# Attention inside a transformer block: weight subtractions in pieces, a copied key half, softmax sums moved into the head's norm

## The chip, the cores and the metric

The kernel runs on one core of a Trainium2 chip. The metric is the time of one execution in device microseconds, the median of several runs. One of the executions is also recorded by the hardware profiler: for every engine it shows when each instruction began and how long it took, and which event ended its wait. Engines are named as the profile names them: PE (TensorE, matrix products and transposes), DVE (VectorE), ACT (ScalarE), POOL (GpSimd) and SP (SyncE, whose queue starts the transfers of weights). L12 is line 12 of the kernel.

## What is computed

One transformer block on 512 tokens of width 1024, in float32. A normalized input is projected by one wide matrix into the queries, keys and values of a differential attention of 8 heads, the latents of a second attention of 8 heads (MLA), and two gates. The first attention weighs two softmax maps, the second with a factor, and normalizes each head's output:

```python
for q, k, c in zip(q_maps, k_maps, coefs):        # coefs = [1.0, -lam]
    s = jnp.einsum('bqhd,bkhd->bhqk', q[:, q0:q1], k[:, :q1], ...) * scale
    p = jax.nn.softmax(jnp.where(mask, s, -jnp.inf), axis=-1) * c
    w = p if w is None else w + p
...
o = rms_norm(o, subln_g) * (1.0 - lambda_init)    # over the 128 columns of a head
```

The gated outputs of both attentions are added, multiplied by w_o and added to the input; then a router picks 2 of 32 experts for each token, in 4 groups, and the experts' gated feed-forward networks (1024 to 512 to 1024) are added.

## The kernel before

**Two-part products.** Matrix products of the attention keep nearly full float32 precision by splitting each operand into a high part, rounded to the matrix engine's format (F32R), and a low part, the rest. `mm3` (L89) then makes three products. `load_split` (L287) does this for weights: SP's queue brings a piece `wraw` of 128 rows by several slices k of n columns (usually four slices of 256 columns, 1024 elements a partition), ACT casts it to `whi` (L298), POOL subtracts, `wlo = wraw - whi` (L299). There are two buffers of `wraw` and four each of `whi` and `wlo`. 72 such pieces are loaded up to some 530 us; other widths are 704, 768, 512 and 384.

**Stages.** ORDER is a string of steps in program order: `q`, `k`, `v` project queries, keys and values of two heads at once; `fq`, `fk` normalize and rotate them (`rope`, L350; `rsqrt`, L95, makes 1/sqrt by a shift, a constant and three rounds of Newton's iteration in a dozen small DVE operations); `st` transposes them and splits them into stacks (`da_stacks`, L481); `h` is one head (`da_head`, L508); `sub` the norms of four heads together (`subln`, L530); `g` and `mg` gates; names with m the same for the second attention; `wo` the first part of the output product. Then come the router and the experts, in 16 pairs, whose weights stream through a ring of buffers by SP's queue (L879). A scheduler takes the program order and, by its own estimate of times, sets the order of instructions on every engine; waits between engines are semaphores derived from what the instructions read and write.

**The keys' stack.** For each of two maps `da_stacks` writes the key's high part twice, into both halves of the 128 partitions (two ACT operations, L501 and L502, out of PSUM), and the low part twice (two DVE operations, L504, also out of PSUM).

**The softmax.** `attend` (L362) goes through four query tiles of 128. For each tile and map PE makes the scores `pss`, DVE adds the mask and takes the row's extreme `nm` (L378), ACT makes the exponentials `e` and their sums `l` (L382). Then DVE takes reciprocals `r` of both sums (L387), multiplies the second by the factor `nlam` (L391), scales the second map (L392), and combines it with the first, scaled in the same operation (L393). PE transposes the result (L398), ACT and DVE split it into `pth` and `ptl` (L82, L83 in `split`), and PE multiplies by the values (L91 to L93). For the second attention, with one map, there is only a reciprocal and one scaling (L395).

**The norm of the heads.** Each head's output `po` is copied, squared and summed over its columns by a product with ones; after four heads `subln` transposes the four sums into a PSUM tile `pt`, `rsqrt` turns them into factors (L100 is its first operation), and each head is scaled.

Of the kernel before, what the change touches and what calls it, by code (L numbers as in the profile page):

```python
# [11 lines left out]
F32 = mybir.dt.float32  # L12
# [10 lines left out]
P = 128  # L23
T = 512
NT = T // P
# [4 lines left out]
EPS = 1e-6  # L30
# [38 lines left out]
class Kernel:  # L69
# [24 lines left out]

    def rsqrt(self, ss, n, scale, pool, tag, out=None):  # L95

        v = self.v
        tags = tag and (tag + "x", tag + "y", tag + "a")
        x, y, a = pool if tag is None else (pool.tile([P] + n if isinstance(n, list) else [P, n], F32, tag=tg, name="rs") for tg in tags)
        v.tensor_scalar(x, ss, scale, EPS, op0=mult, op1=add)  # L100
        yi = y.bitcast(I32)
# [160 lines left out]
    def attention(self):  # L262
# [24 lines left out]
        def load_split(src, nk, n, step, then=(), into=None):  # L287

            w, then = [], list(then)
            for k0 in range(0, nk, step):  # L290
                k1 = min(nk, k0 + step)
                hi = wp.tile([P, k1 - k0, n], F32R, tag="whi", name="whi", bufs=4)
                lo = wp.tile([P, k1 - k0, n], F32R, tag="wlo", name="wlo", bufs=4)
                raw = wp.tile([P, k1 - k0, n], F32, tag="wraw", name="wraw", bufs=2) if into is None else into
                self.last_load = nc.sync.dma_start(raw, src(k0, k1))
                if then:
                    then.pop(0)()
                s.copy(hi, raw)  # L298
                g.tensor_tensor(lo, raw, hi.bitcast(F32), op=sub)  # L299
                w += [(hi[:, k, :], lo[:, k, :]) for k in range(k1 - k0)]  # L300
            return w
# [59 lines left out]

        def attend(scores, scale, vh, vl, po):  # L362
            for hf in range(2):
# [5 lines left out]
                for qi in range(2):  # L369
# [4 lines left out]
                    for m, sc in enumerate(scores):  # L374
# [7 lines left out]
                        s.activation(e[:, 0:nk], pss[:, 0:nk], AF.Exp, scale=-1.0, bias=nm,  # L382
                                     accum_out=l[:, m:m + 1])
                        es.append(e)
                    r = sm.tile([P, 2], F32, tag="r", name="r", bufs=6)
                    n = len(scores)
                    v.reciprocal(r[:, 0:n], l[:, 0:n])  # L387
                    w = es[0][:, 0:nk]
                    if n == 2:
                        e2 = es[1][:, 0:nk]  # L390
                        v.tensor_tensor(r[:, 1:2], r[:, 1:2], self.nlam, op=mult)  # L391
                        v.tensor_scalar(e2, e2, r[:, 1:2], None, op0=mult)  # L392
                        v.scalar_tensor_tensor(w, w, r[:, 0:1], e2, op0=mult, op1=add)  # L393
                    else:
                        v.tensor_scalar(w, w, r[:, 0:1], None, op0=mult)  # L395
                    pt = tps()
# [84 lines left out]
        def da_stacks(hh, q, k):  # L481
# [16 lines left out]
            for m in range(2):  # L498
# [3 lines left out]
                s.activation(kh[b], pk[a], AF.Copy, scale=gk[a])  # L502
                for c in (a, b):
                    v.scalar_tensor_tensor(kl[c], pk[a], gk[a], kh[a].bitcast(F32), op0=mult, op1=sub)  # L504
                ks.append((kh, kl))
            return qs, ks

        def da_head(pr, hh, qs, ks, vv):  # L508
# [9 lines left out]
            po = ps.tile([P, T], F32, tag="O", name="po")  # L518
            attend([mk(0), mk(1)], 64 ** -0.5, lambda kt: vv[0][:, kt, hc], lambda kt: vv[1][:, kt, hc], po)
            o2 = main.tile([P, T], F32, tag="e", name="o2", bufs=4)  # L520
# [3 lines left out]
            pe.matmul(pso[0:32], self.ones, o2, start=True, stop=True)  # L524
            j = h % 4
            if j == 0:
# [3 lines left out]
        def subln(h0):  # L530
# [3 lines left out]
            ss = pt.rearrange("p t (j c) -> p t j c", j=4)[:, :, :, 0]  # L534
            r = self.rsqrt(ss, [NT, 4], 1.0 / P, sm, "rn")
            for j in range(4):
# [793 lines left out]
```

## Time and profile before

| | |
|---|---|
| median of 3 runs | 1081.29 us (1081.0 to 1082.02) |
| profiled execution | 1079.62 us, of which the recorded span is 1077.9 us |
| PE busy | 974.9 us (90%) |
| DVE busy | 512.3 us (48%) |
| ACT busy | 371.5 us (34%) |
| POOL busy | 204.4 us (19%) |
| mean granted clock of PE | 0.959 of full speed |
| DMA, mean over the span | 236 GB/s |

The shares are means over stages that differ: DVE does most of its work before 530 us, the transfers of the experts' weights fill the time after it. A line of the profile that groups instructions gives their number, the busy time in all, the mean of one, and the idle time of the engine in front of them with the instruction that ended it. A row of the timeline gives start, duration, engine, line, operation, the tile written and those read, and the shape; in brackets stands idle time in front of it.

### The profile page before, as it was taken

How to read it: one execution, taken by the hardware profiler on the slowest of the kernel's cores; microseconds unless marked ns; L12 is line 12 of the kernel's file. 1: busy time of each engine (PE TensorE's matmuls, PEld its weight loads, DVE VectorE, ACT ScalarE, POOL GpSimd, SP SyncE). 2: the span in 40 equal slices, each digit the busy share in tenths (PEclk: the TensorE clock that was granted, in tenths of full speed). 3: DMA queues.
4: the chain of work that ended last, by engine and by line, in shares of the span. 5: the costliest groups of instructions: out<-in, count | busy, mean ns of one | idle time of the engine just before them, and what ended most of it. 6: DMA issues, size and time to landing. Idle time of an engine off the chain costs nothing. (4 is left out here: it accounts for less than half of the span.)

```text
span 1077.9 us, 15395 instructions
## 1 busy us (share of the span) xinstructions
PE 974.9 (90%) x5718; PEld 687.1 (64%) x5718; DVE 512.3 (48%) x1512; ACT 371.5 (34%) x783; POOL 204.4 (19%) x218
## 2 busy tenths in 40 slices
PE   6798999999899799989989799999697979969795
PEld 6798988999678688879975354455252633525233
DVE  3878597694969889796463221211030110301012
ACT  5465555746765556645171111101010101101010
POOL 5333233313423222322230000000000000000001
PEclk9999999999999999999979899999898989989898
DMA  6321222112311211244687999999999999999995
GB/s 173 115 79 40 79 79 79 41 42 67 101 48 53 62 54 38 59 163 148 280 320 317 399 377 417 408 403 402 401 401 402 419 402 404 403 402 402 421 356 180
DMA packets 83708, 254.25 MB, mean 236 GB/s; under 512 B 12464, under 2 KB 47024, under 8 KB 65968
## 3 DMA queue, kind: packets, MB, share of 16 engines
q1 hardware_dynamic: 77504, 238.56, 57.6%
q0 software_dynamic: 2704, 9.96, 4.2%
q10 hardware_dynamic: 3424, 4.72, 1.2%
q8 instruction: 46, 0.75, 0.3%
q14 instruction: 30, 0.25, 0.1%
HBM read 240.64 MB, written 12.58 MB: 235 GB/s over the span
## 5 line engine op out<-in xcount | busy, mean ns | idle before, releaser
L1152 PE MATMUL pw<-w,xT 128*64 128x512 f32 x1024 | 250.4, 619 | 39.1 <-DMA w<-in_w_dram 36.7
L1152 PEld LDWEIGHTS pw<-w,xT 128*64 128x64 f32 x1024 | 81.8, 142 | 198.5 <-issue 155.9
L299 POOL TENSOR_TENSOR wlo<-wraw,whi 128x1024 fp32r<-128x1024 f32 (+4 forms) x70 | 149.6, 2147 | 233.9 <-ACT whi L298 233.0
L1161 DVE TENSOR_TENSOR hg<-pw,hg 128x512 f32<-128x512 f32 x16 | 16.7, 1041 | 277.3 <-PE pw L1152 276.5
L91 PE MATMUL pmm<-whi,hTh 128*128 128x256 f32 (+1 forms) x448 | 129.9, 293 | 2.1 <-ACT raw L465 1.8
L92 PE MATMUL pmm<-wlo,hTh 128*128 128x256 f32 (+1 forms) x448 | 129.2, 290 | 0.0
L93 PE MATMUL pmm<-whi,hTl 128*128 128x256 f32 (+1 forms) x448 | 127.2, 291 | 0.0
L1180 PE MATMUL py<-w,hT 128*64 128x512 f32 (+1 forms) x544 | 115.4, 572 | 1.4 <-ACT hT L1166 1.4
L1209 POOL DMA_INDIRECT obuf<-y,rows x15 | 23.5, 1570 | 462.8 <-DVE y L1184 136.3
L91 PEld LDWEIGHTS pmm<-whi,hTh 128*128 128x128 f32 x448 | 85.0, 190 | 3.5 <-ACT raw L465 2.2
L92 PEld LDWEIGHTS pmm<-wlo,hTh 128*128 128x128 f32 x448 | 85.2, 190 | 1.9 <-issue 1.7
L93 PEld LDWEIGHTS pmm<-whi,hTl 128*128 128x128 f32 x448 | 83.7, 190 | 1.1 <-issue 0.8
L1160 ACT ACTIVATE hg<-pw 128x512 f32<-128x512 f32 x16 | 17.0, 1064 | 194.8 <-PE pw L1152 156.7
L1180 PEld LDWEIGHTS py<-w,hT 128*64 128x64 f32 x544 | 42.5, 138 | 65.4 <-issue 56.9
L298 ACT CAST whi<-wraw 128x1024 fp32r<-128x1024 f32 (+4 forms) x70 | 65.0, 931 | 21.4 <-DMA wraw<-in_w_in_dram 6.1
L382 ACT ACTIVATE e<-pss,nm 128x128 f32<-128x128 f32 (+3 forms) x96 | 50.7, 532 | 62.5 <-DVE nm L378 32.3
L1166 ACT COPY hT<-pt 128x512 f32<-128x512 f32 x16 | 9.4, 586 | 163.6 <-PE pt L1164 163.6
L1020 PE MATMUL pg<-sel,hTh 128*128 128x256 f32 x256 | 65.6, 293 | 0.0
L1021 PE MATMUL pg<-sel,hTl 128*128 128x256 f32 x256 | 64.2, 290 | 0.0
L1184 DVE TENSOR_SCALAR y<-py,ws 128x512 f32<-128x512 f32 x15 | 11.2, 747 | 87.2 <-PE py L1180 87.2
L93 PE MATMUL pg<-hTh,wlo 128*128 128x512 f32 x128 | 51.1, 399 | 0.0
L91 PE MATMUL pg<-hTh,whi 128*128 128x512 f32 x128 | 50.9, 398 | 0.0
(344 smaller groups left out, 1920.0 us busy)
## 6 DMA issues: line engine op xcount, KB each, us to landing
w<-in_w_dram SPq DMA_DIRECT2D x138, 1024.0 KB, 16.8
w<-in_w_dram SPq DMA_DIRECT2D x106, 512.0 KB, 14.7
wraw<-in_w_in_dram SPq DMA_DIRECT2D x38, 512.0 KB, 3.7
wraw<-in_w_in_dram SPq DMA_DIRECT2D x8, 352.0 KB, 4.1
obuf<-X ACTq DMA_DIRECT2D x5, 512.0 KB
wraw<-in_mla_w_ukv_dram SPq DMA_DIRECT2D x4, 512.0 KB
wraw<-in_w_o_dram SPq DMA_DIRECT2D x4, 512.0 KB
X<-in_x_dram SPq DMA_DIRECT2D x4, 512.0 KB
```

Of the source, the lines that this page charges most:

```text
L91: self.pe.matmul(out, a[0], b[0], start=first, stop=False)
L92: self.pe.matmul(out, a[0], b[1], start=False, stop=False)
L93: self.pe.matmul(out, a[1], b[0], start=False, stop=last)
L298: s.copy(hi, raw)
L299: g.tensor_tensor(lo, raw, hi.bitcast(F32), op=sub)
L382: s.activation(e[:, 0:nk], pss[:, 0:nk], AF.Exp, scale=-1.0, bias=nm, accum_out=l[:, m:m + 1])
L1020: self.pe.matmul(pg, self.h2h[:, t, k, :], sel, start=t == 0 and k % 2 == 0, stop=False, skip_group_check=True)
L1021: self.pe.matmul(pg, self.h2l[:, t, k, :], sel, start=False, stop=t == NT - 1 and k % 2 == 1, skip_group_check=True)
L1152: end = pe.matmul(p[i * C:(i + 1) * C], xT[:, k, cols[i]], w(name, i, k), start=k == 0, stop=k == KT - 1)
L1160: s.activation(ha, ph[0][0:R].rearrange("p (a k) -> p a k", k=4), AF.Silu)
L1180: pe.matmul(p[i * C:(i + 1) * C], hT[:, k, i * C:(i + 1) * C], w("w2", i, k, c0, m), start=k == 0, stop=k == 3)
L1209: g.indirect_dma_start(self.obuf, bass.IndirectOffsetOnAxis(ap=rows, axis=0), yy, None, bounds_check=T + P - 1, compute_op=add)
```

## The change

Three things are changed. In `load_split` POOL's one subtraction for a loaded piece becomes one for each of its slices k: 72 instructions become 232, of 256 columns mostly (176), and of 128, 352, 384 or 512 where the loads are of that width. In `da_stacks` DVE makes the keys' low part once for each map, and ACT copies it to the other half of the partitions (new line L508). In `attend`, for the first attention, the first map is no longer divided by its sum: its sums go to a tile `l4` that is kept for four heads (one buffer), the second map is multiplied by `l1 * nlam / l2` and added to the unscaled first one in a single operation. As the head's output is then too large by the factor l1, and a norm follows that divides by the root of the mean square plus EPS, only EPS has to be multiplied by l1 squared: `subln` makes `EPS * l4 * l4`, and `rsqrt` adds that in place of the constant. The functions below keep their order otherwise; lines of the new kernel are some 3 to 9 higher.

```diff
@@ -92,12 +92,15 @@
         self.pe.matmul(out, a[0], b[1], start=False, stop=False)
         self.pe.matmul(out, a[1], b[0], start=False, stop=last)
 
-    def rsqrt(self, ss, n, scale, pool, tag, out=None):
+    def rsqrt(self, ss, n, scale, pool, tag, out=None, eps=None):
 
         v = self.v
         tags = tag and (tag + "x", tag + "y", tag + "a")
         x, y, a = pool if tag is None else (pool.tile([P] + n if isinstance(n, list) else [P, n], F32, tag=tg, name="rs") for tg in tags)
-        v.tensor_scalar(x, ss, scale, EPS, op0=mult, op1=add)
+        if eps is None:
+            v.tensor_scalar(x, ss, scale, EPS, op0=mult, op1=add)
+        else:
+            v.scalar_tensor_tensor(x, ss, scale, eps, op0=mult, op1=add)
         yi = y.bitcast(I32)
         v.tensor_scalar(yi, x.bitcast(I32), 1, None, op0=OP.logical_shift_right)
         v.tensor_scalar(yi, yi, -1.0, 1597463007.0, op0=mult, op1=add)
@@ -296,7 +299,8 @@
                 if then:
                     then.pop(0)()
                 s.copy(hi, raw)
-                g.tensor_tensor(lo, raw, hi.bitcast(F32), op=sub)
+                for k in range(k1 - k0):
+                    g.tensor_tensor(lo[:, k], raw[:, k], hi[:, k].bitcast(F32), op=sub)
                 w += [(hi[:, k, :], lo[:, k, :]) for k in range(k1 - k0)]
             return w
 
@@ -359,7 +363,9 @@
             v.tensor_tensor(out, xv, tb(cg, 0, 2 * h), op=mult)
             v.tensor_tensor(out, out, b, op=add)
 
-        def attend(scores, scale, vh, vl, po):
+        def attend(scores, scale, vh, vl, po, l0=None):
+
+
             for hf in range(2):
                 nkt = 2 * hf + 2
                 pth = main.tile([P, nkt, 256], F32R, tag=f"pth{hf}", name="pth")
@@ -380,19 +386,17 @@
                                                op0=add, op1=OP.min, accum_out=nm)
                         e = main.tile([P, T], F32, tag="e", name="e", bufs=4)
                         s.activation(e[:, 0:nk], pss[:, 0:nk], AF.Exp, scale=-1.0, bias=nm,
-                                     accum_out=l[:, m:m + 1])
+                                     accum_out=l[:, m:m + 1] if l0 is None or m else l0[qt])
                         es.append(e)
                     r = sm.tile([P, 2], F32, tag="r", name="r", bufs=6)
-                    n = len(scores)
-                    v.reciprocal(r[:, 0:n], l[:, 0:n])
                     w = es[0][:, 0:nk]
-                    if n == 2:
-                        e2 = es[1][:, 0:nk]
-                        v.tensor_tensor(r[:, 1:2], r[:, 1:2], self.nlam, op=mult)
-                        v.tensor_scalar(e2, e2, r[:, 1:2], None, op0=mult)
-                        v.scalar_tensor_tensor(w, w, r[:, 0:1], e2, op0=mult, op1=add)
+                    if l0 is None:
+                        v.reciprocal(r[:, 0:1], l[:, 0:1])
+                        v.tensor_scalar(w, w, r[:, 0:1], None, op0=mult)
                     else:
-                        v.tensor_scalar(w, w, r[:, 0:1], None, op0=mult)
+                        v.reciprocal(r[:, 0:1], l[:, 1:2])
+                        v.scalar_tensor_tensor(r[:, 1:2], r[:, 0:1], l0[qt], self.nlam, op0=mult, op1=mult)
+                        v.scalar_tensor_tensor(w, es[1][:, 0:nk], r[:, 1:2], w, op0=mult, op1=add)
                     pt = tps()
                     for kt in range(qt + 1):
                         pe.transpose(pt[:, kt, :], w[:, kt * P:(kt + 1) * P], ident)
@@ -500,8 +504,8 @@
                 kh, kl = stk("kh"), stk("kl")
                 s.activation(kh[a], pk[a], AF.Copy, scale=gk[a])
                 s.activation(kh[b], pk[a], AF.Copy, scale=gk[a])
-                for c in (a, b):
-                    v.scalar_tensor_tensor(kl[c], pk[a], gk[a], kh[a].bitcast(F32), op0=mult, op1=sub)
+                v.scalar_tensor_tensor(kl[a], pk[a], gk[a], kh[a].bitcast(F32), op0=mult, op1=sub)
+                s.copy(kl[b], kl[a].bitcast(F32))
                 ks.append((kh, kl))
             return qs, ks
 
@@ -516,13 +520,16 @@
                     pe.matmul(p[:, 0:n], qq, ks[m][1][:, 0:n], start=False, stop=True)
                 return sc
             po = ps.tile([P, T], F32, tag="O", name="po")
-            attend([mk(0), mk(1)], 64 ** -0.5, lambda kt: vv[0][:, kt, hc], lambda kt: vv[1][:, kt, hc], po)
+            j = h % 4
+            if j == 0:
+                self.l4 = sm.tile([P, NT, 4], F32, tag="l4", name="l4", bufs=1)
+            attend([mk(0), mk(1)], 64 ** -0.5, lambda kt: vv[0][:, kt, hc], lambda kt: vv[1][:, kt, hc], po,
+                   [self.l4[:, t, j:j + 1] for t in range(NT)])
             o2 = main.tile([P, T], F32, tag="e", name="o2", bufs=4)
             s.activation(o2, po, AF.Square)
             s.copy(mixed[:, h, :], po)
             pso = ps.tile([P, T], F32, tag="O", name="pso")
             pe.matmul(pso[0:32], self.ones, o2, start=True, stop=True)
-            j = h % 4
             if j == 0:
                 self.s4 = dp.tile([P, T], F32, tag="s4", name="s4")
             s.copy(self.s4[32 * j:32 * j + 32], pso[0:32])
@@ -532,7 +539,9 @@
             for t in range(NT):
                 pe.transpose(pt[:, t, :], self.s4[:, t * P:(t + 1) * P], ident)
             ss = pt.rearrange("p t (j c) -> p t j c", j=4)[:, :, :, 0]
-            r = self.rsqrt(ss, [NT, 4], 1.0 / P, sm, "rn")
+
+            v.scalar_tensor_tensor(self.l4, self.l4, EPS, self.l4, op0=mult, op1=mult)
+            r = self.rsqrt(ss, [NT, 4], 1.0 / P, sm, "rn", eps=self.l4)
             for j in range(4):
                 pb = ps.tile([P, T], F32, tag="O", name="pb")
                 for t in range(NT):
```

The scheduler places the new instructions. On DVE, for the first query tile of head 0, from a pair of key operations to the combination of the two maps, there stands before:

```order
L504 SCALAR_TENSOR_TENSOR kl<-pt,dagck,kh 64x512 x2
L378 ISA pss,nm<-pss,mask 128x256
L378 ISA nm 128x1
L387 RECIPROCAL r<-l 128x2
L426 TENSOR_REDUCE ssq<-sq 128x4
L391 TENSOR_TENSOR r<-r,nlam 128x1
L602 TENSOR_TENSOR ssq<-ssq,rx_343 128x16
L392 TENSOR_SCALAR e<-e,r 128x128
L100 TENSOR_SCALAR rs<-ssq 128x16
L393 SCALAR_TENSOR_TENSOR e<-e,r 128x128
```

and now (L507 is the key operation, L384 mask and extreme, L397 the reciprocal, L398 the factor, L399 the combination, L101 the first operation of `rsqrt`):

```order
L507 SCALAR_TENSOR_TENSOR kl<-pt,dagck,kh 64x512
L384 ISA pss,nm<-pss,mask 128x256
L384 ISA nm 128x1
L397 RECIPROCAL r<-l 128x1
L398 SCALAR_TENSOR_TENSOR r<-r,l_851,nlam 128x1
L399 SCALAR_TENSOR_TENSOR e<-e,r 128x128
L430 TENSOR_REDUCE ssq<-sq 128x4
L611 TENSOR_TENSOR ssq<-ssq,rx_355 128x16
L101 TENSOR_SCALAR rs<-ssq 128x16
```

The combination stands two places behind the reciprocal, where it stood six places behind; the sums of the projection (L430) and the small operations of the norm come after it.

On DVE, some 290 us into the kernel, heads 6 and 7 run beside the second attention's first steps. There stands before, from the copy of a rotated key (L591) to an operation of a norm's Newton iteration behind a pair of key operations:

```order
L591 COPY krd<-ckv 128x512
L111 TENSOR_TENSOR rs<-rs 128x4
L113 SCALAR_TENSOR_TENSOR rs<-rs 128x4
L378 ISA pss,nm<-pss,mask 128x128
L378 ISA nm 128x1
L112 TENSOR_TENSOR rs<-rs 128x4
L582 TENSOR_TENSOR r_4031<-rs 128x4
L113 SCALAR_TENSOR_TENSOR rs<-rs 128x4
L111 TENSOR_TENSOR rs<-rs 128x4
L112 TENSOR_TENSOR rs<-rs 128x4
L504 SCALAR_TENSOR_TENSOR kl<-pt,dagck,kh 64x512 x2
L113 SCALAR_TENSOR_TENSOR rs<-rs 128x4
```

and now (L600 is the copy, L116, L114 and L115 the Newton iteration, L101 to L107 its beginning, L507 the key operation):

```order
L600 COPY krd<-ckv 128x512
L116 SCALAR_TENSOR_TENSOR rs<-rs 128x4
L507 SCALAR_TENSOR_TENSOR kl<-pt,dagck,kh 64x512
L591 TENSOR_TENSOR r_4106<-rs 128x4
L101 TENSOR_SCALAR rs<-ssc 128x4
L105 TENSOR_SCALAR rs<-rs 128x4
L106 TENSOR_SCALAR rs<-rs 128x4
L107 TENSOR_SCALAR rs<-rs 128x4
L384 ISA pss,nm<-pss,mask 128x256
L384 ISA nm 128x1
```

One key operation is gone, and the beginning of the next norm stands where the steps of two norms alternated before.

## Rows read from the trace of the kernel before

**Rows 1.** Busy time by stretch: length; busy us (instructions) of PE, PEld, DVE, ACT, POOL; clock; DMA; GB/s.
```profile
75.00:100.00 25.00, 21.19 (x167) 20.09 (x166) 24.51 (x75) 10.71 (x26) 7.15 (x5) 1.00 0.30 85
...
275.00:300.00 25.00, 19.47 (x89) 15.02 (x88) 24.36 (x66) 17.08 (x40) 10.50 (x5) 0.87 0.33 88
...
600.00:700.00 100.00, 92.28 (x500) 45.44 (x497) 23.11 (x79) 12.30 (x19) 6.50 (x4) 0.97 1.01 399
```

**Rows 2.** Waits of PE behind 560 us: in all, times, longest (us).
```profile
PE pw L1152 <- DMA w<-in_w_dram: 36.7, 12, 7.9
```

**Rows 3.** Waits of PE from 25 to 530 us; twenty rows, the first four and last.
```profile
PE pss L515 <- ACT e L382: 6.3, 6, 4.5
PE pt L398 <- DVE e L393: 4.2, 4, 1.7
PE pt L487 <- DVE raw L360: 4.0, 1, 4.0
PE po L92 <- DVE ptl L83: 3.2, 1, 3.2
...
PE po L91 <- ACT pth L82: 0.2, 1, 0.2
```

**Rows 4.** Timeline of POOL and DVE, 72 to 95 us: start, duration (us).
```profile
72.21 4.76 POOL L299 TENSOR_TENSOR wlo<-wraw,whi 128x1024 fp32r<-128x1024 f32 x2 [10.10 <-ACT whi L298]
...
74.67 2.38 DVE L392 TENSOR_SCALAR e<-e,r 128x128 f32<-128x128 f32 x1
...
92.15 2.33 DVE L100 TENSOR_SCALAR rs<-ssk 128x16 f32<-128x16 f32 x1
```

**Rows 5.** Timeline of DVE, 285 to 297 us.
```profile
287.92 2.37 DVE L111 TENSOR_TENSOR rs<-rs 128x4 f32<-128x4 f32 x1
...
292.69 1.80 DVE L113 SCALAR_TENSOR_TENSOR rs<-rs 128x4 f32<-128x4 f32 x1
```

**Rows 6.** Timeline of POOL and DVE, 346 to 352 us.
```profile
345.98 5.84 POOL L299 TENSOR_TENSOR wlo<-wraw,whi 128x1024 fp32r<-128x1024 f32 x2 [6.87 <-ACT whi L298]
...
347.11 2.52 DVE L356 TENSOR_TENSOR ropeb<-mq,mqts 128x256 f32<-128x256 f32 x1
```

**Rows 7.** Timeline of DVE, first and last held instruction.
```profile
22.11 2.37 DVE L111 TENSOR_TENSOR rs<-rs 128x4 f32<-128x4 f32 x1
...
512.54 1.51 DVE L395 TENSOR_SCALAR e<-e,r 128x512 f32<-128x512 f32 x1
```

**Rows 8.** Groups of instructions up to 560 us: count, busy us, mean ns, idle before.
```profile
L299 POOL TENSOR_TENSOR wlo<-wraw,whi 128x1024 fp32r<-128x1024 f32 x46 | 113.1, 2468 | 175.5 <-ACT whi L298 175.5
...
L299 POOL TENSOR_TENSOR wlo<-wraw,whi 128x512 fp32r<-128x512 f32 x8 | 10.8, 1355 | 12.6 <-ACT whi L298 12.6
...
L504 DVE SCALAR_TENSOR_TENSOR kl<-pt,dagck,kh 64x512 fp32r<-64x512 f32 x32 | 24.0, 749 | 9.1 <-ACT kh L502 8.7
...
L661 ACT CAST qr<-pt 64x512 fp32r<-64x512 f32 x8 | 4.6, 579 | 3.2 <-DVE qr L662 1.8 <-PE pt L646 1.2
...
L392 DVE TENSOR_SCALAR e<-e,r 128x128 f32<-128x128 f32 (+3 forms) x32 | 18.7, 585 | 0.5
```

**Rows 9.** Timeline of POOL and DVE, 40 to 46 us.
```profile
40.62 5.17 POOL L299 TENSOR_TENSOR wlo<-wraw,whi 128x1024 fp32r<-128x1024 f32 x2 [5.42 <-ACT whi L298]
...
41.09 2.39 DVE L112 TENSOR_TENSOR rs<-rs 128x16 f32<-128x16 f32 x1
...
43.40 0.41 DVE L426 TENSOR_REDUCE ssk<-sq 128x4 f32<-128x256 f32 x1
...
43.73 2.10 DVE L113 SCALAR_TENSOR_TENSOR rs<-rs 128x16 f32<-128x16 f32 x1
...
45.86 0.17 DVE L111 TENSOR_TENSOR rs<-rs 128x16 f32<-128x16 f32 x1
```

**Rows 10.** Timeline of ACT and DVE, 211 to 214 us.
```profile
211.06 0.37 ACT L382 ACTIVATE e<-pss,nm 128x128 f32<-128x128 f32 x1
...
213.67 0.17 DVE L100 TENSOR_SCALAR rs<-pt 128x16 f32<-128x16 f32 x1 [0.20 <-PE pt L533]
```

## The prediction

> **What bounds the kernel now.** I read three views in this order: the engines' busy time by stretch, the waits of PE, and the timeline of POOL and DVE in front of those waits. From about 575 us on the kernel is the mixture of experts, and there the DMA queues are the bound: in the stretch 600 to 700 us the 16 DMA engines are busy throughout (share 1.01) while PE is busy 92.3 of 100 us [rows 1], and PE's longest total wait behind 560 us is 36.7 us on the expert weights [rows 2]. The change touches nothing there. Expert weights begin to flow when the attention's weights are through, so whatever the attention ends earlier or later is passed on to the end one for one; the loads' order differs little, and I allow 1 us either way.
>
> So the change is worth what PE's idle time between 25 and 530 us is worth. PE does the same matmuls before and after. Its named waits there are a short list: 6.3 us for an exponential of ScalarE (six waits, one of 4.5), 4.2 for the combined weights e, 4.0 once for a rotated key, 3.2 once for ptl, down to 0.2 in the twentieth row [rows 3]; the twenty make 31.5 us, and that is the ceiling of any gain in this part. Where these waits stand, DVE is full: 24.51 of 25 us busy in 75 to 100 while PE is busy 21.19, and 24.36 in 275 to 300, where PE has 19.47 and a granted clock of 0.87 [rows 1].
>
> Why DVE is full there is seen in the timeline. At 74.67 a DVE multiplication of 128x128 takes 2.38 us; POOL's subtractions of two weight halves run from 72.21 to 76.97, so the DVE instruction ends about when POOL's second does. At 92.15 a tiny 128x16 operation takes 2.33 us [rows 4]; its like at 45.86 takes 0.17 [rows 9]. Transposes of PE wait for e behind both. At 287.92 a 128x4 operation takes 2.37 us and at 292.69 another takes 1.80 [rows 5], in front of PE's 4.5 us wait for an exponential. At 347.11 a rope operation of 128x256 takes 2.52 us under a double subtraction of 5.84 [rows 6], the next one as long under the rest of it; the wait for ptl follows. Compared with the shortest of their like, 38 of the 72 subtractions hold one DVE instruction each, 57 us in all, the first at 22.11 and the last at 512.54 [rows 7]. What is held reads or writes two operands in SBUF; instructions that read PSUM run through. The Trainium skill ("SBUF — State Buffer", "Reading the diagram") calls the pair of ports that DVE and GpSimd share an exclusive lock for the whole instruction, whose loser blocks fully; the trace agrees, with 2.38 beside 2.4 us.
>
> **The change part by part.**
>
> *Pieces of the subtraction.* A 1024-column half takes 2468 ns (46 of them), a 512-column one 1355 [rows 8]: 2.17 ns a column and 0.24 us for each instruction. A piece of 256 columns is then 0.80 us by these two rows; bounds are a quarter of 2468, 0.62, and the whole 512 row, 1.36. By 0.80 the 72 subtractions become 232 pieces, and POOL works 160 x 0.24 = 39 us longer; it stood waiting for ScalarE most of the time, and its weights are needed some us after the cast, so this lies beside other work. What changes for DVE is the longest hold: 2.4 us becomes at most 0.8, if DVE gets a turn between two POOL instructions. The trace shows that it does: a held operation (41.09, 2.39 us) ends within the double row of subtractions at 40.62 that runs to 45.79, a reduction starts at 43.40, and the next held one (43.73, 2.10) lasts to that row's end [rows 9]. But a chain of DVE operations that all want the same ports then meets a new piece at each step. The gain is therefore in stretches where DVE mixes kinds, and a loss is possible where it runs such chains back to back.
>
> *One softmax pass less.* The first map's sums are no longer divided out; e is combined as e1 + (l1·nlam/l2)·e2 in one operation. L392 goes, 32 instructions, 18.7 us with its holds; the small multiplication L391 becomes one with a second factor, at the same price [rows 8]. The head's norm needs the sums squared: two small operations more, 0.2 us each by the tiny ones. In DVE's order for the first query tile one instruction stands between the reciprocal and the combination where five stood, so e is ready sooner.
>
> *Keys' lower half.* 16 of 32 L504 at 749 ns go: 12.0 us of DVE. ScalarE gets 16 casts of 64x512 SBUF to SBUF; the nearest row is a cast of that shape out of PSUM, 579 ns [rows 8], so 9.3 us, spread over engine time in which ScalarE is busy 10.7 and 17.1 of 25 us [rows 1]. Each puts 0.6 us in front of an exponential in ScalarE's queue if it falls badly, and the copy adds one hand-over to the keys' path; I take the hand-over as hidden behind the exponentials that precede a head's first score, and 0 to 1 us in all if that cover is gone.
>
> *A new wait.* The first sums of heads 4 to 7 are written where the norm of heads 0 to 3 still reads. Head 4's first exponential ran at 211.06, and the norm's first operation on DVE at 213.67 [rows 10]: 2.6 us too early. It now waits; behind it on ScalarE stand the squares and copies of the next projection, and for those PE's buffers. The new order puts head 4's scores some 3 us later, with projection matmuls ahead, so PE has work. Price 0, and up to 2.6 us if it has not.
>
> **The sum**, by places where PE waits:
> - A, waits for e (4.2 us, four waits). The held L392 is gone and holds are 0.8 at most: +3.6 (2.0 to 4.2).
> - B, waits for exponentials (6.3, six waits). The 4.5 is behind 2.37 and 1.80 us of held tiny operations and a pair of L504, of which one stays. Holds shrink by 1.6 and 1.0 and 0.75 goes, 3.3 of 4.5; small ones stay: +3.2 (1.0 to 6.0).
> - C, the wait for ptl (3.2). Two holds of about 2.1 each become 0.4 to 0.8: +2.9 (1.5 to 3.2).
> - D, the start. Between 25 and 50 us DVE runs chains of 128x16 operations on SBUF in front of the 4.0 us wait [rows 3], while 44 pieces stream through POOL nearly back to back. Each step can meet a piece: in the stretch 40.62 to 45.8 two steps were held 4.2 us altogether; with eight pieces, 6.4 us of POOL time, some eight steps meet one each for 0.4 to 0.8: 3.2 to 6.4. I take -1.7 (-3.5 to 0).
> - E, the clock. The stretch 275 to 300 runs at 0.87 while 75 to 100 runs at 1.00 [rows 1]: 0.13 x 19.5 us busy is 2.5 us if it never falls. The fall comes after PE's idle, so half goes with B: +1.0 (0 to 2).
> - F, everything else, the new wait, the ScalarE casts, the MLA stage with its full DVE: 0 (-2.6 to +1.5).
>
> Together 3.6 + 3.2 + 2.9 - 1.7 + 1.0 = 9.0 us. The profiled execution took 1079.62 us, 1.7 under the median of 1081.29; the sum is made in it, 1070.6, and against the median it gives 1072.3. All low ends together give 4.5 - 6.1 = -1.6, all high ends +16.9.
>
> On the piece's price the Trainium skill ("GPSIMD Engine Reference", section 3.1) has 2.6 cycles per element of a two-input operation and 4497 ns for 2048 columns, which leaves hardly anything per instruction: an estimate of about 0.6 us for 256 columns. By it D would be some 0.5 us better and the time 1071.8; no run here shows that width yet.
>
> **The rivals.**
> 1. *Given back.* The attention stages gain as above, but MLA's stage, where DVE is as full, loses through ScalarE and DVE queues what is gained: A and B in half, C gone to the next wait, D full: 1.8 + 1.6 - 1.7 + 1 = 2.7, so 1078.6. For it: PE's waits are on many different tiles behind 300 us, each small. Against: L392 and L504 leave 30 us of DVE time outright. 0.20.
> 2. *All of it.* A, B and E in full, C 3.2, D near 0, since the pieces interleave well: 4.2 + 6.3 + 2.0 + 3.2 = 15.7, so 1065.6. For it: the held operations are mostly tiny, and under a short piece little of them is left. Against: the startup chains. 0.14.
> 3. *Slower: pieces hold more.* With 232 pieces DVE meets the ports more often. Now 57 of POOL's 155 us of subtracting are holds, 37%. With 193 us of pieces, DVE is even when the holds reach 57 + 29 (what softmax and keys free) = 86 us, 45%. At 55% it loses 20 us; with a third of that on PE's path, as 30 us of idle stand now against some 90 us of holds and removed work, 1081.3 + 6.7 = 1088. For it: two held steps in the one dense double subtraction [rows 9]; against: 34 of 72 subtractions hold nothing, and DVE's mix has PSUM readers in it. 0.10.
> 4. *Not what it says.* POOL keeps the ports through a row of queued pieces, so holds stay 2.4 us: then A and B gain only by what leaves DVE, a third of 29 us at most and nothing at C: about 5 us, 1076. Against it stands the turn at 43.40 [rows 9]. 0.06.
>
> **How the numbers follow.** Forecast 0.50, and 0.20, 0.14, 0.10, 0.06 for the rivals: 1072.3 us. The range goes from rival 2 with its upper bound less a little, 1064, to 1080.5, which holds rivals 1 and 4 and leaves out the slower one. About 0.2%, 2.2 us, is what a measurement here tells from no change: 1079.1 to 1083.5 is "same". Of the forecast 0.04 lies there, of rival 1 0.07 with 0.01 more behind it, and 0.02 of rival 3: same 0.13; slower 0.08 + 0.01 = 0.09; faster 0.78.
>
> **What would show it.** Right: no DVE instruction of 128x16 or 128x4 longer than 1 us beside a subtraction; PE's waits for e under 1 us in all, for ptl under 0.8; the stretch 275 to 300 with PE above 22 and clock near 1.00. D right: PE's idle in 25 to 50 us grows by one to three us. Wrong, if the total of holds goes up, if PE waits on ScalarE's cast of the keys or on head 4's first exponential for over 1 us, or if the attention's end moves and the end of the kernel does not.

## The result and the profile after

The changed kernel takes **1069.85 us** (median of 4 runs, 1069.64 to 1073.73) where the kernel before takes 1081.19 (4 runs); the ratio is 0.990 with a 95% interval of 0.9882 to 0.9918. The forecast was 1072.3 us with a range of 1064.0 to 1080.5. The profiled execution took 1069.64 us, its span is 1067.6.

Busy time by stretch of the changed kernel, with the columns of [rows 1]:

```profile
25.00:50.00 25.00, 19.82 (x159) 19.01 (x160) 19.29 (x77) 11.59 (x24) 12.62 (x16) 1.00 0.42 124
75.00:100.00 25.00, 24.37 (x192) 22.87 (x191) 21.59 (x72) 14.85 (x35) 8.94 (x17) 1.00 0.25 75
275.00:300.00 25.00, 20.42 (x94) 16.22 (x94) 23.81 (x75) 20.29 (x46) 11.41 (x16) 0.86 0.29 87
600.00:700.00 100.00, 92.78 (x490) 45.72 (x492) 22.07 (x74) 11.75 (x19) 5.21 (x4) 0.97 1.01 397
```

From 75 to 100 us PE is busy 24.37 us instead of 21.19, and DVE 21.59 instead of 24.51. From 275 to 300 little has changed, and the clock is 0.86 where it was 0.87. The experts' stretch is as it was, with the DMA engines full.

PE's waits from 25 to 530 us are now 22 rows and 23.8 us (before 20 rows and 31.5), beside [rows 3]:

```profile
PE pt L491 <- DVE raw L364: 3.3, 1, 3.3
PE pt L585 <- DVE th L416: 2.5, 1, 2.5
PE pss L519 <- ACT e L388: 2.4, 3, 1.0
...
PE pt L402 <- DVE e L399: 1.3, 3, 0.6
```

The wait for ptl is gone, those for exponentials fell from 6.3 to 2.4 and those for e from 4.2 to 1.3; the wait for a rotated key only from 4.0 to 3.3, and a wait of 2.5 in front of transposes (L585), ended by a DVE operation of a gate (L416), is new.

The groups that answer to [rows 8]: pieces, key operations, copies, and the new factor:

```profile
L303 POOL TENSOR_TENSOR wlo<-wraw,whi 128x256 fp32r<-128x256 f32 x176 | 130.3, 773 | 133.0 <-ACT whi L301 132.8
...
L507 DVE SCALAR_TENSOR_TENSOR kl<-pt,dagck,kh 64x512 fp32r<-64x512 f32 x16 | 12.0, 748 | 13.1 <-ACT kh L506 12.9
...
L508 ACT CAST kl<-kl 64x512 fp32r<-64x512 f32 x16 | 9.9, 618 | 0.7 <-DVE kl L507 0.2
L398 DVE SCALAR_TENSOR_TENSOR r<-r,l,nlam 128x1 f32<-128x1 f32 x32 | 8.5, 265 | 0.7
```

The first products of the experts began at 573.75 us before and begin at 563.35 now, 10.4 us sooner (timeline of PE); the span is 10.3 us shorter.

```profile
563.35 16.96 PE L1161 MATMUL pw<-w,xT 128*64 128x512 f32 x78
```

So the experts' part itself gives and takes nothing.

### The profile page after: what moved, and what is told of

The parts are those of the page before. It is cut to its first block, busy times and chain, and to the rows that moved or that the text cites. A ratio compares the mean times of both kernels' runs of the same rounds, so it can differ in the third digit from the quotient of the medians.

```text
span 1067.6 us, 15556 instructions
## 1 busy us (share of the span) xinstructions
PE 969.9 (91%) x5718; PEld 685.8 (64%) x5718; DVE 480.9 (45%) x1466; ACT 381.6 (36%) x799; POOL 231.4 (22%) x378
## 5 line engine op out<-in xcount | busy, mean ns | idle before, releaser
L303 POOL TENSOR_TENSOR wlo<-wraw,whi 128x256 fp32r<-128x256 f32 (+4 forms) x228 | 176.6, 806 | 205.6 <-ACT whi L301 198.4
L1161 PEld LDWEIGHTS pw<-w,xT 128*64 128x64 f32 x1024 | 84.7, 141 | 195.6 <-issue 158.2
L384 DVE CUSTOM_DVE_ANT_0 pss<-pss,mask 128x128 f32<-128x128 f32 (+3 forms) x96 | 47.0, 495 | 19.5 <-PE pss L520 15.8
```

The source lines that it names most:

```text
L303: g.tensor_tensor(lo[:, k], raw[:, k], hi[:, k].bitcast(F32), op=sub)
L384: v.tensor_tensor_reduce(out=pss[:, 0:nk], in0=pss[:, 0:nk], in1=self.mask[:, 512 - nk:512], scale=-scale, scalar=3e38, op0=add, op1=OP.mi ...
L1161: end = pe.matmul(p[i * C:(i + 1) * C], xT[:, k, cols[i]], w(name, i, k), start=k == 0, stop=k == KT - 1)
```

## How the runs are compared

The table shows one profiled execution of each kernel, and the ratio of its timed median to that of the kernel before on the same chip. **Holds** are the DVE instructions that last over 0.15 us longer than the lower quartile of their like while a subtraction of POOL runs that ends no later than they do: their number, the excess in all, and the longest. Counting every excess above 0.05 us changes little (46 us for the changed kernel, 35 for half slices, 57 before). **Lead** is PE's progress: each of its matmuls is priced by the usual gap to the next one in the trace before, and the lead is by how much sooner the work that the kernel before had done at 540 us is done. The changed kernel and e12 have the same order in the attention, and leads of 10.3 and 9.4: so much two executions differ. Leads, and sums and differences of them, are read with that in mind.

| kernel | holds | us in all | longest us | lead us | ratio (95%) |
|---|---|---|---|---|---|
| before | 38 | 57.3 | 2.23 | 0 | 1 |
| changed | 93 | 45.2 | 1.12 | 10.3 | 0.990 (0.9882 to 0.9918) |
| e1 pieces only | 92 | 44.8 | 1.09 | 7.4 | 0.9922 (0.9905 to 0.994) |
| e2 keys only | 41 | 60.7 | 2.22 | -3.6 | 0.9979 (0.9969 to 0.999) |
| e3 softmax only | 38 | 55.9 | 2.23 | -0.3 | 1.0008 (0.9997 to 1.0019) |
| e4 softmax and keys | 43 | 60.2 | 2.26 | 3.0 | 0.9907 (0.9891 to 0.9924) |
| e5 pieces and softmax | 81 | 40.6 | 1.12 | 5.6 | 0.9905 (0.9871 to 0.994) |
| e9 pieces and keys | 95 | 45.6 | 1.09 | 7.7 | 0.9872 (0.9849 to 0.9895) |
| e6 changed, two slices | 55 | 50.5 | 1.61 | 7.2 | 0.9897 (0.9866 to 0.9929) |
| e11 changed, half slices | 120 | 31.2 | 0.65 | 16.6 | 0.9795 (0.9774 to 0.9816) |
| e8 changed, whole at the start | 75 | 45.5 | 2.25 | 12.5 | 0.9892 (0.986 to 0.9924) |
| e7 before, no subtraction | 0 | 0 | 0 | 32.4 | 0.9656 (0.9627 to 0.9685) |
| e10 changed, no subtraction | 0 | 0 | 0 | 28.2 | 0.9696 (0.9673 to 0.9719) |
| e12 changed, other order of late loads | 91 | 44.7 | 1.12 | 9.4 | 0.9907 (0.9889 to 0.9926) |

Theory A is the forecast's: DVE, held by POOL, is late in front of PE, and the pieces carry the gain. Theory B: DVE's busy time as such, of which softmax and keys free most.

## The experiments

**e1, pieces only.** In the kernel before:

```diff
-                g.tensor_tensor(lo, raw, hi.bitcast(F32), op=sub)
+                for k in range(k1 - k0):
+                    g.tensor_tensor(lo[:, k], raw[:, k], hi[:, k].bitcast(F32), op=sub)
```

> The kernel before with the subtraction in pieces of one slice and nothing else. Theory A (what counts is how long a single DVE instruction in front of PE is held, up to 2.2 us before): pieces alone bring the larger half of the 11 us. The ptl wait (3.2 us) goes, the waits for e fall from 4.2 to about 2, the 4.5 us wait for an exponential loses about 2: 1074 to 1076 us. Theory B (what counts is DVE's busy time in all, since the holds of the changed kernel still add up to 45 us where 57 were): 12 of 43 us saved, a quarter of the gain, 1078 to 1079 us.

Measured: 1072.15 us beside 1081.53 for the kernel before on that chip, 9.4 us of the gain, more than A asked and far from B's 1078. The lead is 7.4 us. Pieces could help in another way too: the products of a first slice need not wait for the whole subtraction. But no row of PE's waits from 25 to 530 us names POOL, in the kernel before, in this one or in the changed one, so PE was not waiting for lower parts.

**e2, keys only.** In the kernel before:

```diff
-                for c in (a, b):
-                    v.scalar_tensor_tensor(kl[c], pk[a], gk[a], kh[a].bitcast(F32), op0=mult, op1=sub)
+                v.scalar_tensor_tensor(kl[a], pk[a], gk[a], kh[a].bitcast(F32), op0=mult, op1=sub)
+                s.copy(kl[b], kl[a].bitcast(F32))
```

> The kernel before with the key's lower half copied by ScalarE and nothing else: 12 us of DVE less, 9 us of ScalarE more. Theory A: the holds stay, only the pair in front of the 4.5 us wait is shortened by 0.75: 1079 to 1081 us. Theory B: 12 of 43 us saved, 1078 us. A third one, that the hand-over costs what the copy saves: 1081 us or more, with new PE waits on key tiles.

Measured: 1079.27 us, 2.3 faster by the times, but not by the attention: PE is 3.6 us late at its end, and the experts' part, as it was scheduled here, took some 3.7 us less. DVE had 12 us less to do; the holds rose to 60.7 us. The timeline of POOL, DVE and PE shows one of the places where the attention lost:

```profile
164.20 2.50 POOL L299 TENSOR_TENSOR wlo<-wraw,whi 128x1024 fp32r<-128x1024 f32 x1 [8.30 <-DVE e L392]
```
```profile
164.41 2.71 DVE L393 SCALAR_TENSOR_TENSOR e<-e,r 128x384 f32<-128x384 f32 x1
```
```profile
167.27 0.52 PE L398 MATMUL pt<-ident,e 128*128 128x128 f32 x3 [2.01 <-DVE e L393]
```

In the new order the subtraction begins 0.2 us ahead of a combination, which is held to the subtraction's end (166.70), and PE waits 2.0 us. The kernel before has no such meeting there. Here, then, what an edit of DVE's work did depended on which instructions met a long subtraction afterwards.

**e3, softmax only.** The kernel before with the changes in `attend`, `da_head`, `subln` and `rsqrt` alone:

```diff
-                        v.tensor_scalar(e2, e2, r[:, 1:2], None, op0=mult)
-                        v.scalar_tensor_tensor(w, w, r[:, 0:1], e2, op0=mult, op1=add)
+                        v.scalar_tensor_tensor(r[:, 1:2], r[:, 0:1], l0[qt], self.nlam, op0=mult, op1=mult)
+                        v.scalar_tensor_tensor(w, es[1][:, 0:nk], r[:, 1:2], w, op0=mult, op1=add)
```

> The kernel before with the first softmax's sums divided out in the head's norm and nothing else: 18.7 us of DVE less, of it 6 to 7 us holds. Theory A: the waits for e lose what L392 itself was held (2.4 us at 74.67), the rest of the holds moves to the next instruction on the same ports: 1078 to 1080 us. Theory B: 18.7 of 43 us saved: 1076 us.

Measured: 1081.87 us beside 1081.53, no change; both theories asked for more. The four removed multiplications of a head leave the holds at 55.9 us, 38 of them as before: others are held in their place. The lead shows it: it grows by 2.5 us between 75 and 100 us, where the held L392 stood, and is lost again by 200 us. At 164.85 us a combination begins 0.1 us behind a subtraction and lasts 2.79 us, and PE waits 2.1 us for it.

**e4, whole subtractions.** The changed kernel with the first diff above undone.

> The changed kernel with whole subtractions again (softmax and keys stay changed). Theory A: the ptl wait and long holds come back, 1075 to 1077 us. Theory B: only a quarter is lost, 1072 to 1073 us.

Measured: 1070.85 us, faster than either theory said. In the attention it does lose: the lead is 3.0 us instead of 10.3, but 2.3 of these 7.3 us are made up before the experts begin, and the experts' part, in another order, takes 2.7 less (first product of the experts 568.3 us, last one 1056.8; in the changed kernel 563.35 and 1054.5). So the timed totals do not tell this kernel from the changed one (0.9907 and 0.990): that pieces pay on top of the other two changes shows in the lead alone.

**e5, pieces and softmax.** The changed kernel with the second diff above undone.

> The changed kernel with DVE making both copies of the keys' lower part again, so pieces and softmax only. Theory A (pieces carry the gain, the freed DVE time little): PE stays 9 to 10 us ahead of the kernel before when the experts begin. Theory B (the 12 us of DVE count once the holds are short): 2 to 3 us less, 7 us ahead. Its order of expert loads ends as in the keys-only kernel, where the last pair came 4 us sooner than the lead at the experts' beginning tells; so the end is 3 to 4 us ahead of that, 1066 to 1068 us by A and 1069 to 1070 by B.

Measured: lead 5.6 us, 1070.54 us beside 1082.28. It lost 4.7 us of lead, more than B's 2 to 3 for the keys, and the total is within the interval of the changed kernel's.

**e9, pieces and keys.** The kernel before with the first two diffs.

> The kernel before with pieces and the copied keys, old softmax. Alone the keys' copy put PE 3.6 us behind at the experts' beginning, with held combinations of 2.4 and 2.7 us in front of PE. Theory A (that loss is the new order meeting long holds): with pieces the copy costs nothing, the lead is 7 to 10 us, at or above the 7.4 of pieces alone. Theory C (the copy's hand-over through ScalarE costs it): 7.4 less 3.6, about 4 us.

Measured: lead 7.7 us, as A said; 1066.37 us beside 1080.64. Theory C asked for 4 us: the copy's hand-over does not cost what it said. This kernel, with the old softmax, is no slower than the changed one (0.9872 and 0.990); its experts' part takes 487.4 us where that of the changed kernel takes 491.2.

The eight kernels with each edit on and off are now complete. **Pieces** add 7.4 us of lead alone, 5.9 beside softmax, 11.3 beside keys, 7.3 beside both: always a gain, 8.0 in the mean. **Keys** add -3.6, 3.3 (beside softmax), 0.3 (beside pieces), 4.7: 1.2 in the mean. **Softmax** adds -0.3, 6.6, -1.8, 2.6: 1.8 in the mean. The last two are not told apart from what a new order does by itself. The times, in the same four places and as differences of ratios, give pieces 0.78, 1.03, 1.07 and 0.07%: about 8, 11, 12 and 1 us. The last one is the pair of e4.

**e6 and e11, other sizes of piece.** The changed kernel with two slices to a piece:

```diff
+                for k in range(0, k1 - k0, 2):
+                    d = slice(k, min(k + 2, k1 - k0))
+                    g.tensor_tensor(lo[:, d], raw[:, d], hi[:, d].bitcast(F32), op=sub)
```

> The changed kernel with pieces of two slices, 512 columns mostly, so holds up to 1.1 us. If the length of one hold in front of PE counts, it lies between whole subtractions and single slices: a lead of 6 to 8 us at the experts' beginning. If only the number of instructions on POOL or the sum of holds counts, no difference from the changed kernel: 10 us.

and with half slices:

```diff
+                for k in range(k1 - k0):
+                    for c in (slice(0, n // 2), slice(n // 2, n)):
+                        g.tensor_tensor(lo[:, k, c], raw[:, k, c], hi[:, k, c].bitcast(F32), op=sub)
```

> The changed kernel with pieces of half a slice, 128 columns mostly, 464 of them. Leads at 540 us were 3.0 with whole subtractions, 7.2 with two slices, 10.3 with one. If the longest hold counts, on to 11 to 13 us. If the sum of holds counts (more pieces, a turn lost at each), or POOL's own time does (some 60 us more), under 9 us.

Measured with two slices: a lead of 7.2 us, where the length of a hold asked for 6 to 8, and 1070.27 us beside 1082.28, not told apart from the changed kernel. The sum of holds was expected to stay, but rose from 45.2 to 50.5 us, so that rival is not refuted by it. With half slices: a lead of 16.6 us, more than the 11 to 13 that were asked, and **1058.13 us** (1057.38 to 1060.05) beside 1080.64, a ratio of 0.9795: the fastest kernel here that leaves nothing out. Its span is 11.5 us shorter than the changed kernel's, and 3.4 of these lie in the experts' part (487.8 us where that of the changed kernel takes 491.2). The group of half slices:

```profile
L304 POOL TENSOR_TENSOR wlo<-wraw,whi 128x128 fp32r<-128x128 f32 x352 | 159.3, 491 | 133.8 <-ACT whi L301 120.2 <-PE pss L520 4.9 <-PE pmm L93 4.8
```

and PE's waits from 25 to 530 us, 15 rows of 19.2 us in all:

```profile
PE pt L586 <- DVE cTk L86: 3.5, 1, 3.5
...
PE pt L492 <- DVE raw L365: 1.9, 1, 1.9
```

POOL works longer (239 us on subtractions where one slice took 189 and whole ones 155), but still sits idle for 120 us until casts of ScalarE end, and DVE is held 31.2 us instead of 45.2. The rival, that a turn is lost at each piece and the sum of holds rises, does not come about: the number of holds rises from 93 to 120, but in the mean they are half as long.

**e7 and e10, no subtraction.** What holds cost in all, in the kernel before and in the changed one:

```diff
-                g.tensor_tensor(lo, raw, hi.bitcast(F32), op=sub)
+                g.memset(lo[:, 0, 0:1].bitcast(F32), 0.0)
-                w += [(hi[:, k, :], lo[:, k, :]) for k in range(k1 - k0)]
+                w += [(hi[:, k, :], hi[:, k, :]) for k in range(k1 - k0)]
```

> The kernel before without POOL's subtractions: the lower parts of the weights are left out, and the products that read them read the upper part again (same matmuls, other values). It measures all that the holds cost. If the 57 us of holds are what PE waits for in front of its waits, the lead at the experts' beginning is 12 to 16 us, and the waits for e, for the 4.5 us exponential and for ptl go. If PE's waits come from DVE's own work, under 5 us.

> The changed kernel without POOL's subtractions: the weights' lower parts are left out, the products read the upper part again. Beside the kernel before without them (lead 32 us at 540 us, 1044 us) it shows what softmax and keys are worth when nothing holds DVE. Theory A: DVE is then no bound in front of most waits, so 0 to 3 us more. Theory B (their 31 us of DVE time count by themselves): 5 us more or above, under 1040 us.

Measured: 1044.2 and 1048.3 us, leads of 32.4 and 28.2. The first is twice the 12 to 16 that were expected: PE's waits from 25 to 530 us shrink to 12 rows and 12 us, the waits for e, for a rotated key and for ptl are gone, those for exponentials fall from 6.3 to 0.7, and the start alone gives 5 us by 50 us. It is a ceiling, since it also takes away whatever else hangs on the subtractions, such as the buffers that they free. The second decides against B: without holds, softmax and keys leave DVE 26 us less to do (its instructions add up to 514.8 instead of 541.0 us over the whole execution) and PE gains nothing, not even the 0 to 3 us of A: it is 4 us later. Why it is later is not shown.

Put side by side, the changed kernel with whole, two-slice, one-slice, half-slice and no subtractions has 60.2, 50.5, 45.2, 31.2 and 0 us of holds and leads of 3.0, 7.2, 10.3, 16.6 and 28.2. A line through the two ends gives 0.42 us of lead for each us of hold, and 7.1, 9.3 and 15.1 for those between: within 1.5 us of what was measured. The kernel before gives 32.4 / 57.3 = 0.57, by which e1's 12.5 us less would be 7.1; it has 7.4. So along this series PE's progress goes with the **sum** of the holds; the longest hold goes with it too (2.26, 1.61, 1.12 and 0.65 us), and nothing here separates the two fully. e8 comes nearest: five holds of 1.7 to 2.25 us remain in it, the sum is 45.5, and its lead is no smaller than the changed kernel's. Between kernels whose other edits differ the sum does not give the order: e5 has 40.6 us of holds and a lead of 5.6, e9 45.6 and 7.7. And in time whole, two-slice and one-slice pieces are not told apart (0.9907, 0.9897, 0.990); only half slices stand out.

**e8, whole at the start.** The changed kernel with whole subtractions for its first 13 loads:

```diff
+                self.nload = getattr(self, "nload", 0) + 1
+                d = k1 - k0 if self.nload <= 13 else 1
+                for k in range(0, k1 - k0, d):
+                    g.tensor_tensor(lo[:, k:k + d], raw[:, k:k + d], hi[:, k:k + d].bitcast(F32), op=sub)
```

> The changed kernel with whole subtractions for the first 13 loads (to some 90 us) and pieces from there. By term D of the forecast the pieces cost 1.7 us in the start: then the lead at 50 us of work is larger than the changed kernel's 1.1, at 2 to 3. Rival: the pieces help there too, as the changed kernel's trace suggests; then the lead at 50 us is 0 to 0.5 and at 100 us 1 to 4 us smaller than the changed kernel's 5.7.

Measured: the lead at 50 us is 0.1 us and at 100 us 1.9, where the changed kernel has 1.1 and 5.7. The lead at 50 us is as the rival said, but there e12, with the changed kernel's order, has 0.6, so that figure alone decides little. At 100 us e12 has 4.7, and the rival holds: pieces help in the start too. This kernel's order differs from the changed one's, and between 275 and 300 us it gains more; its time, 1069.22 us, is not told apart from the changed kernel's.

**e12, order of late loads.** In `load`, the third matrices of the last but one pair are put behind the first two of that pair:

```diff
+                    with ExitStack() as after:
+                        for d in self.w13 if pair and name == "w2" else ():
+                            after.enter_context(self.tc.issue_after(d.ins))
+                        self.last_w = dma(t0, src)
```

> The changed kernel, with the last loads of expert weights put in the order that the keys-only kernel had: the first two matrices of the last but one pair before its third. There the last pair ended 3 to 4 us sooner after the experts' beginning (488 us against 491). If that is the order of loads: 1066 to 1067 us, with the same attention. If it was something else: 1070 us.

Measured: 1069.79 us (6 runs, 1067.39 to 1072.93), no gain in the times. In the profiled execution the time from the experts' first product to their last is 487.8 us instead of 491.2. Not settled: that execution was the fastest of six, and e9 has 487.4 with another order of these loads. What makes the experts' part last 488 us in some kernels and 491 in others stays open; timed totals of kernels whose late order differs carry these 3 us.

## Why the prediction was right

- **One for one to the end.** The first product of the experts moved by 10.4 us, the span by 10.3. That held for this change; e2 and e4, whose experts' part took 3.7 and 2.7 us less, show that it need not. The prediction allowed 1 us for the order of late loads; whether that order is the cause stays open (e12).
- **The mechanism.** Pieces shorten holds, DVE gets its turns between them, and pieces alone bring most of the gain (e1); half slices bring more, and no subtraction the most (e11, e7). A piece was put at 0.80 us; the mean is 0.773. A hold was put at 0.8 us at most; the longest is 1.12, beside a piece of 512 columns at 341.64 us. POOL's extra time was put at 39 us; it is 189 less 155, 34. The estimate of 0.6 us from the Trainium skill ("GPSIMD Engine Reference", section 3.1) is further off: an instruction of POOL does carry a fixed share, since 352 pieces of 128 columns take 491 ns each, not half of 773. The two means give about 2.2 ns a column and 0.2 us for each instruction.
- **Term A, waits for e.** Forecast +3.6; the lead grows by 3.8 us between 75 and 100 us (from 1.9 to 5.7), and the waits by name fell by 2.9. In this stretch pieces alone gain 2.9 (e1) and softmax alone 2.5 (e3).
- **Term C, the wait for ptl.** Forecast +2.9; the wait is gone, and the lead grows from 6.6 to 9.8 us between 350 and 400.
- **Terms B and E, exponentials and clock.** Forecast +4.2 together. The waits for exponentials did fall by 3.9, but the lead grows by only 0.6 from 275 to 325 us (5.7, 8.4 at 300, 6.3), and PE waits 2.5 in front of L585 in their place. This is rival 1, given back, in one place: PE's idle in 275 to 300 us is still 4.6 us. The step of E that failed is that half of the clock's loss goes with B. Of the clock's two levels the lower one, 1.2 GHz, lasts 6.80 us before and after; it began inside PE's idle time of 4.53 us before, and begins 0.9 us behind the wait of 2.5 now. Before, PE was idle for half of it, and now it works through nearly all of it (columns of [rows 1], before and after):

```profile
293.30:300.10 6.80, 3.44 (x13) 2.90 (x14) 6.73 (x23) 4.49 (x12) 2.99 (x2) 0.50 0.15 33
```
```profile
289.50:296.30 6.80, 6.09 (x22) 5.06 (x23) 6.18 (x20) 6.53 (x15) 1.97 (x2) 0.50 0.23 61
```

  If half of PE's busy time at this level is lost to the clock, it cost 1.7 us before and costs 3.0 now, an estimate from these two rows: 1.3 us more, where the forecast had 1.0 less.
- **Term D, the start.** Forecast -1.7; the lead is 1.1 us at 50 us and 1.9 at 75, and PE's idle in 25 to 50 us falls from 6.4 to 5.2 where it was to grow by one to three. In each of the four pairs of kernels with and without pieces the lead at 75 us is larger with them, by 0.2 to 2.9 us. One premise was misread: 44 pieces were to stream through POOL there nearly back to back. The row of the kernel before has four subtractions, so 16 pieces, and in the changed kernel they keep POOL busy for 12.62 of 25 us:

```profile
25.00:50.00 25.00, 18.61 (x151) 18.03 (x152) 19.64 (x75) 10.83 (x23) 9.92 (x4) 1.00 0.44 129
```

  The timeline of POOL and DVE that answers to [rows 9]:

```profile
40.35 6.99 POOL L303 TENSOR_TENSOR wlo<-wraw,whi 128x256 fp32r<-128x256 f32 x8 [4.30 <-ACT whi L301]
```
```profile
40.83 0.73 DVE L115 TENSOR_TENSOR rs<-rs 128x16 f32<-128x16 f32 x1
41.48 0.41 DVE L430 TENSOR_REDUCE ssk<-sq 128x4 f32<-128x256 f32 x1
41.81 0.44 DVE L116 SCALAR_TENSOR_TENSOR rs<-rs 128x16 f32<-128x16 f32 x1
42.29 0.66 DVE L114 TENSOR_TENSOR rs<-rs 128x16 f32<-128x16 f32 x1
42.98 0.66 DVE L115 TENSOR_TENSOR rs<-rs 128x16 f32<-128x16 f32 x1
43.67 0.66 DVE L116 SCALAR_TENSOR_TENSOR rs<-rs 128x16 f32<-128x16 f32 x1
44.37 0.66 DVE L614 TENSOR_TENSOR rs<-rs,rx 128x16 f32<-128x16 f32 x1
```

  The chain does meet a piece at each step, as forecast: DVE and POOL take turns, steps last 0.66 us instead of 0.17, and the holds from 25 to 50 us add up to 5.0 us where 4.1 were. But that sum replaces the old one. The step that ran at 45.86 before (L111, [rows 9]) runs at 42.29 here (L114), and the chain's last link (L614) ends at 45.03, sooner than that. The step that failed is the difference of the two sums: 3.2 to 6.4 against 4.2 was taken as a loss of 1.7; the sums differ by 0.9 over the stretch, and the chain in front of PE came sooner all the same.
- **What the sum left out.** The lead rises by 2.6 us between 150 and 175 us and falls by 1.9 until 275; the sum had nothing there. D was wrong by 3.6 the one way, B and E together by 3.6 the other. That they cancel is luck, and so is part of the closeness of the total: 9.0 us were forecast, 10.0 lie between the profiled executions and 11.3 between the medians.
- **The ceiling.** The 31.5 us of PE's named waits were called the ceiling of any gain. They are not: without subtractions PE gains 32.4 us with 12.0 of waits left (e7).
- **Softmax and keys.** Priced rightly as instructions (keys 12.0 us of DVE, casts 618 ns where 579 was taken from the nearest row), but the sum gave them a share in A and B that does not last: over the whole attention each alone brings nothing that can be told from a new order, and without holds the two together bring nothing at all (e10).
- **The signs.** The holds fell, the wait for ptl went and the end followed the attention, as asked. Missed are: waits for e under 1 us in all (1.3), PE above 22 us in 275 to 300 (20.42), a clock near 1.00 there (0.86), and no operation of 128x4 above 1 us (one of 1.24 at 286.68).
- **The new wait.** Price 0, as forecast. Head 4's first exponential on ACT and the norm's first operation on DVE, which answer to [rows 10]:

```profile
206.84 0.38 ACT L388 ACTIVATE e<-pss,nm 128x128 f32<-128x128 f32 x1
```
```profile
205.26 0.17 DVE L103 SCALAR_TENSOR_TENSOR rs<-pt,l 128x16 f32<-128x16 f32 x1 [1.88 <-PE pt L540]
```

  The norm has read the old sums 1.6 us before the exponential begins, and there is no idle time in front of the latter.
- **Rival 3**, holds at 45% of POOL's time and above: they are 45.2 of 189 us, 24%, and 13% with half slices. **Rival 4**, no turns between pieces: the longest hold is 1.12 us, beside pieces of up to 512 columns; refuted. **Rival 2**, all of it, falls with B and E.

## What to carry to other kernels

Where two engines shut each other out for whole instructions, cut the instructions of the one that has time to spare, and go on cutting while the sum of holds falls: here it fell to 128 columns, though each instruction carried about 0.2 us of its own. Measure the holds and PE's progress at the end of the stage, not the total alone: most edits here came with a new order of the scheduler's, which moved the attention by up to some 4 us (e2, e3) and went with a last stage 3 us shorter or longer. That is more than two of the three edits were worth in the mean. Work taken from an engine that is busy all the time need not help; what stood in PE's way was when that engine got its turn.

## What the runs showed of the hardware that was not expected

Tiny DVE operations on SBUF and POOL's pieces alternate one for one. From 42.29 us on, four steps in the rows above start at a pitch of 0.69 us; the single pieces of POOL's merged row start at 42.18, 42.88, 43.57 and 44.26 us and last 0.73, and each step ends with the piece that it met. With half slices (e11) the same steps have a pitch of 0.42 us. POOL is held as well: its piece at 45.63 us lasts 1.71, beside a DVE operation of 128x1024 at 45.06.

Which DVE instructions are held is as clear in the kernel before: of those that began over 0.3 us ahead of a subtraction's end, 48 read PSUM and none was held, nor any of 13 sums over columns (L426) and 7 reciprocals (L387), which read one tile of SBUF.

The cost of holding reaches beyond PE's named waits. Without subtractions PE has done by 507.6 us what it had done by 540. Of these 32.4 us, 22.8 are idle time (38.8 before, 16.0 without subtractions) and 9.6 are busy time (501.2 and 491.6). The lower clock level accounts for some of the latter: in these stretches it lasts 17 us before and 7 without subtractions, at most 5 us by the estimate above. The rest is open.
